# Experts of the second block's mixture: output copies, width of the weight rounding, and order of the third product's passes

## The chip, the cores and the metric

The kernel runs on one core of a Trainium2 chip. The metric is the device time of one execution in microseconds (us), as the median of several executions. TensorE (PE) multiplies, VectorE (DVE), ScalarE (ACT) and GpSimd (POOL) work on elements, and the sync engine (SP) and POOL issue transfers. [...]

## The reference

The program is two transformer blocks in a row over one sequence of 2,048 tokens with a width of 1,024, in float32. The change lies in the second block's mixture of experts, cut to what matters here:

```python
# 32 experts, D = 1024, hidden width 256, two experts for each token
h = rmsnorm(x, norm_ffn_g)
g_top, g_idx = top_k(softmax(h @ w_rg + b_rg), 1)          # one of 4 groups
e_top, e_idx = top_k(softmax(e_in), 2)                     # two of its 8 experts
wts = g_top * e_top / sum(e_top)
def expert(xb, e):
    return (silu(xb @ w_g[e]) * (xb @ w_u[e])) @ w_d[e]    # three products
x = x + sum over the token's two experts of wts * expert(h, e)
```

## The kernel before

The whole program keeps float32 precision by parts. A number is written as a high part, rounded to TensorE's short format (fp32r), and a low part, the rest. `split` (L68 to L77) makes them: ACT copies the source into the high part (L73), and a subtraction on DVE, or on POOL where it is told so, makes the low part (L74). A product is then three passes on PE, which `mm3` issues (L80 to L85): high by high (L83), high by low (L84), low by high (L85). In the rows the operand named first behind the arrow is the one that streams, so `py<-dh,al` is the pass with the low part of the activations.

`phase_k` runs the 32 experts one after the other. Each expert has a list of token rows. A tile takes its first 128 rows, and a second tile of 64 rows is run if the expert has more than 128 (experts with over 192 would go through a loop ahead, which this data doesn't enter). For each expert x there are two versions of a block in the program, and a register chooses one: the full block with the second tile, and the else block without it. In this data 16 of the 32 blocks are full: 0 to 6, 16, 17, 19, 21 to 25 and 28.

In block x stand, in the program's order:

- for a full block, the second rows' hidden layer, `hidden2`, on PE (tile `g2`, 16 passes), with its own small chain on ACT and DVE (tile `t2`, shown as `t`; L2137 to L2141);
- the first rows' hidden layer, `hidden` (tile `g1`, 24 passes of 512 columns: gate in the first 256 columns, up in the others);
- between its passes, called by `beside`: the transposes of the next expert's rows (`turn1`, L2093, two of them, each split by ACT into `xh` and by DVE into `xl`), in odd blocks also those of the next second rows (`turn2`, L2108, tile `x2`, shown as `x`), and the transposes of the last expert's hidden layer (`out_a`, L2147, split into `ah` and `al`);
- the third product of the expert before, `out_b`: two PSUM tiles `py` of 512 columns, six passes each, copied to `y` (L2160 by ACT, L2162 by DVE), which POOL then scatters to memory (L2084);
- rounding work for the next expert: `split_in` makes the parts `gh` (ACT) and `gl` (DVE) of its gate and up weights from the loaded tile `raw`, 4,096 columns in all; `split_down` makes the parts `dh` (ACT) and `dl` (POOL) of its down weights from the loaded tile `sd`, 2,048 columns in all;
- for a full block, the second rows' third product, `out2_b` (8 passes, ACT copy L2180 and DVE add L2181).

Transposes take one of three PSUM buffers `pt`, in turn. In an odd block two `turn1` and one `turn2` come ahead of `out_a`, so `out_a` must wait until the first `turn1` buffer has been read by both its copies. The parts of the weights have two slots each, so an expert's parts are written while the other slot's are multiplied. The order on each engine is settled when the program is built, by a scheduler that models it, so it need not be the order of the code. An engine runs its own list strictly in order. POOL also gathers the next experts' rows (L2081).

Of the kernel before, what the change touches and what calls it, by code (L numbers as in the profile page):

```python
# [14 lines left out]
AF = mybir.ActivationFunctionType  # L15
# [49 lines left out]
def f32(ap):  # L65
    return ap.bitcast(F32)


def split(e, hi, lo, src, scale=None, eng=None):

    nc = e.nc
    if scale is None:
        nc.scalar.activation(hi, src, AF.Copy)  # L73
        (eng or nc.vector).tensor_tensor(lo, src, f32(hi), op=ALU.subtract)  # L74
    else:
        nc.scalar.activation(hi, src, AF.Copy, scale=scale)
        nc.vector.scalar_tensor_tensor(lo, src, scale, f32(hi), op0=ALU.mult, op1=ALU.subtract)  # L77


def mm3(e, out, a, b, start, stop):  # L80

    t = e.nc.tensor
    t.matmul(out, a[0], b[0], start=start, stop=False)  # L83
    t.matmul(out, a[0], b[1], start=False, stop=False)  # L84
    t.matmul(out, a[1], b[0], start=False, stop=stop)  # L85
# [1911 lines left out]
    V.tensor_scalar(tok, ti, 1, None, op0=ALU.arith_shift_right)  # L1997


KW = 2  # L2000


def phase_k(e, last, keep, tiles):
# [9 lines left out]
    nc, tc, d = e.nc, e.tc, e.d  # L2013
# [3 lines left out]
    with ExitStack() as st:  # L2017
# [16 lines left out]
        def half(s, i):  # L2034

            return s.rearrange("p k c -> p (k c)")[:, i * 2048:(i + 1) * 2048].rearrange("p (k c) -> p k c", k=8)
# [6 lines left out]
        def load_down(x, s):  # L2043
            nc.sync.dma_start(s.rearrange("p (k a) c -> p k (a c)", k=2), d["w_down_e_2"][0, x].rearrange("(k p) c -> p k c", p=128))
# [5 lines left out]
        def load_late(i):  # L2050
            if i == 0:
                nc.sync.dma_start(wq, d["w_ple_2"][0].rearrange("(k p) c -> p k c", p=128))
            else:
                nc.sync.dma_start(xq, d["p_2"][0, 0, tiles.start * 128:tiles.stop * 128].rearrange("(t p) c -> p t c", p=128))

        def split_in(w, s, x):

            for i in range(2):
                c = slice(i * 256, i * 256 + 256)
                for k in range(0, 8, KW):  # L2060
                    k = slice(k, k + KW)
                    split(e, w[0][:, k, c], w[1][:, k, c], half(s, i)[:, k])
                    if k.stop == 8 and x < 32:
                        load_in(x, s, i)
                    elif k.stop == 8 and i == 1:
                        e.load_gate(x % 2)
                    yield

        def split_down(w, s, x):
            for k in range(2):  # L2070
                for i in range(2):
                    c = slice(i * 512, (i + 1) * 512)
                    split(e, w[0][:, k, c], w[1][:, k, c], s[:, 2 * k + i], eng=nc.gpsimd)
                    if k == i == 1 and x < 32:
                        load_down(x, s)
                    elif k == i == 1:
                        load_late(x % 2)
                    yield

        def gather(tok, xr):  # L2080
            nc.gpsimd.indirect_dma_start(out=xr, out_offset=None, in_=HF, in_offset=bass.IndirectOffsetOnAxis(ap=tok, axis=0))  # L2081
# [1 line left out]
        def scatter(y, dst):  # L2083
            nc.gpsimd.indirect_dma_start(out=Y, out_offset=bass.IndirectOffsetOnAxis(ap=dst, axis=0), in_=y, in_offset=None,  # L2084
                                         bounds_check=2 * S - 1, oob_is_err=False)
# [13 lines left out]
        def turn1(xr, x, parts=(0, 1)):  # L2099
            turn(xr, lambda j: x[0][:, 4 * j:4 * j + 4], lambda j: x[1][:, 4 * j:4 * j + 4], parts)  # L2100

        def turn2(xr, x2, parts=(0, 1)):

            for j in parts:
                p = pt.tile([128, 4, 128], F32, name="pt")
                for i in range(4):
                    k = 4 * j + i
                    nc.tensor.transpose(p[:, i, :], xr[:, k * 128:(k + 1) * 128], e.ident)  # L2108
                pv = p.rearrange("p i (e c) -> p i e c", e=2)
                h, l = (x2[:, 4 * j:4 * j + 4, :, q, :] for q in range(2))  # L2110
                split(e, h, l, pv)
# [4 lines left out]
        def hidden(w, x, sg, beside=lambda k: None):  # L2116

            g = pg.tile([128, 512], F32, name="g1")
            for k in range(8):
                mm3(e, g, (x[0][:, k], x[1][:, k]), (w[0][:, k], w[1][:, k]), k == 0, k == 7)  # L2120
                beside(k)
            nc.scalar.activation(sg, g[:, :256], AF.Silu)
            nc.vector.tensor_mul(sg, sg, g[:, 256:])
# [8 lines left out]
        def hidden2(w, x2, i):  # L2132
            g = pg.tile([128, 512], F32, name="g2")
            for k in range(8):
                both(g, x2[:, k, i], w[0][:, k], w[1][:, k], k == 0, k == 7)
            t = op.tile([64, 512], F32, name="t2", bufs=1)
            nc.scalar.activation(t, g[64:128], AF.Copy)  # L2137
            nc.vector.tensor_add(t, t, g[0:64])
            sg = t[:, :256]
            nc.scalar.activation(sg, sg, AF.Silu)  # L2140
            nc.vector.tensor_mul(sg, sg, t[:, 256:])  # L2141
            return sg

        def out_a(sg):
            p = pt.tile([128, 4, 128], F32, name="pt")
            for i in range(2):
                nc.tensor.transpose(p[:, i, :], sg[:, i * 128:(i + 1) * 128], e.ident)  # L2147
            a = [op.tile([128, 2, 128], F32R, name="a" + n) for n in "hl"]
            split(e, a[0], a[1], p[:, 0:2])
            return a  # L2150

        def out_b(w, a, dst):
            y = op.tile([128, D], F32, name="y")
            for j in range(2):
                yp = py.tile([128, 512], F32, name="py")
                c = slice(j * 512, (j + 1) * 512)
                for k in range(2):
                    mm3(e, yp, (a[0][:, k], a[1][:, k]), (w[0][:, k, c], w[1][:, k, c]), k == 0, k == 1)
                if j == 0:
                    nc.scalar.activation(y[:, c], yp, AF.Copy)  # L2160
                else:
                    nc.vector.tensor_copy(y[:, c], yp)  # L2162
            scatter(y, dst)

        def out2_a(sg):
            p = pt.tile([128, 4, 128], F32, name="pt")
            for i in range(2):
                nc.tensor.transpose(p[:, i, :64], sg[:, i * 128:(i + 1) * 128], e.ident[:64, :64])
            a = op.tile([128, 2, 2, 64], F32R, name="a2")
            split(e, a[:, :, 0], a[:, :, 1], p[:, 0:2, :64])  # L2170
            return a
# [12 lines left out]
        def all_of(g):  # L2184
            for _ in g:
                pass
# [31 lines left out]
        with tc.If(most > 1):  # L2218
            with tc.For_i(0, 32) as x:
                n = nc.values_load(nb[0:1, bass.ds(x, 1)], min_val=0, max_val=17)  # L2220
                with tc.For_i(1, n) as j:
                    xj = sb.tile([128, 2], F32, name="xj")
                    for i, r in enumerate((x, j)):
                        a = RT[bass.ds(r, 1)]
# [9 lines left out]
                    p = pt.tile([128, 4, 128], F32, name="pt")  # L2234
# [10 lines left out]
                    for name, w, k, c in (("w_gate_e_2", W[1], 4, 0), ("w_up_e_2", W[1], 4, 256), ("w_down_e_2", WD[1], 1, 0)):  # L2245
                        src = d[name][0, bass.ds(x, 1)].rearrange("o r c -> (o r) c").rearrange("(k p) c -> p k c" if k == 1 else "(p k) c -> p k c", p=128)
                        for h in range(2):
                            k_, c_ = slice(h * k, (h + 1) * k), slice(c, c + 1024 // k)
                            s = op.tile([128, D], F32, name="y").rearrange("p (k c) -> p k c", k=k)
# [9 lines left out]
        def block(x, second):  # L2259

            y = (x + 1) % 2
            steps = split_in(W[y], RG[y], x + 3) if x < 31 else iter(())
            parts = lambda n: [next(steps, None) for _ in range(n)]
            parts(2)
            if second:
                sg2 = hidden2(W[x % 2], x2, x % 2)
                parts(2)
            a, a2 = [], []

            def beside(k):  # L2270
                if k == OUT and x:
                    a.extend(out_a(SG[x - 1]))
                if k in TURN and x < 31:
                    turn1(XR[(x + 1) % 2], X[x + 1], (TURN.index(k),))
                    if k == TURN[1]:
                        rows(x + 3)
                if k == OUT2 and second:
                    a2.append(out2_a(sg2))
                if k in TURN2 and x % 2 == 1 and x < 31:
                    turn2(xr2, x2, (TURN2.index(k),))  # L2280
                    if k == TURN2[1]:
                        rows2(x // 2 + 2)
                parts(1)

            hidden(W[x % 2], X[x], SG[x], beside)
            if x:
                out_b(WD[(x - 1) % 2], a, e.dst[:, 0, x - 1:x])
            parts(16)
            if x < 31:
                all_of(split_down(WD[y], RD[y], x + 3))  # L2290
            if second:
                out2_b(WD[x % 2], a2[0], e.dst[0:64, 1, x:x + 1])
            if x == 31:
                out_b(WD[x % 2], out_a(SG[x]), e.dst[:, 0, x:x + 1])

        for x in range(32):
# [6 lines left out]
            n = nc.values_load(nb[0:1, 33 + x:34 + x], min_val=0, max_val=33)  # L2303
# [186 lines left out]
```

## Time and profile before

| | |
|---|---|
| median of 3 runs | 3558.35 us (3557.78 to 3562.14) |
| profiled execution | 3560.11 us |
| its span | 3558.4 us |
| mean granted TensorE clock | 0.975 of 2.4 GHz |
| busy share of the span | PE 94%, DVE 68%, ACT 58%, POOL 19% |
| stretch of the 32 expert blocks | 2861.7 to 3327.0 us of the span |

The profile gives busy times by engine and line, the waits (which engine sat idle at which line, and which instruction of another engine ended it), and the instructions in order of time. A row of the order of time has the start, the time from the first start to the last end of the instructions merged in it, the engine, line and operation, the tiles, and in brackets the idle time of the engine before it with what ended it.

### The profile page before, as it was taken

What the parts mean: (1) busy time and instruction counts of PE and PEld (TensorE: products, weight loads), DVE (VectorE), ACT (ScalarE), POOL (GpSimd) and SP (SyncE); (2) the same over time, 40 slices, a digit from 0 to 9 for tenths busy, and PEclk for the clock granted to TensorE, in tenths of its full rate; (3) what the DMA queues carried; (4) which work ended last, traced back from release to release, by engine and by line L of the source; (5) the groups of instructions that cost most, each with busy time, mean ns of one, the idle gap of its engine ahead of it and who ended that gap; (6) DMA issues with size and microseconds to landing.
All of it is one profiled execution on the core that took longest, in us unless ns stands there. A gap on an engine that the chain in (4) does not pass through costs nothing. (4 is left out here: it accounts for less than half of the span.)

```text
span 3558.4 us, 48779 instructions
## 1 busy us (share of the span) xinstructions
PE 3340.2 (94%) x16556; PEld 2592.6 (73%) x16557; DVE 2427.9 (68%) x4600; ACT 2052.8 (58%) x3672; POOL 688.9 (19%) x729
## 2 busy tenths in 40 slices
PE   8999999999999998999986998988999989899798
PEld 6788766666666666889975777766778767677687
DVE  5835768888888865464454887877856657877654
ACT  4442357777777783243223777877833467777533
POOL 0000000000000000000022433433200046655332
PEclk9999999999999998999997999999999989999999
DMA  5333322101111026443247533332255578878753
GB/s 160 102 122 105 95 71 72 51 22 54 34 45 44 26 63 197 146 139 112 75 127 187 106 79 77 84 69 60 83 167 167 211 263 309 342 301 302 276 195 130
DMA packets 312984, 468.82 MB, mean 132 GB/s; under 512 B 66455, under 2 KB 201384, under 8 KB 304416
## 3 DMA queue, kind: packets, MB, share of 16 engines
q1 hardware_dynamic: 293174, 404.26, 36.6%
q0 software_dynamic: 19520, 60.97, 4.7%
q8 instruction: 148, 2.42, 0.3%
q14 instruction: 142, 1.16, 0.1%
HBM read 333.81 MB, written 135.24 MB: 132 GB/s over the span
## 5 line engine op out<-in xcount | busy, mean ns | idle before, releaser
L519 DVE TENSOR_REDUCE mx<-pmx 128x1 f32<-128x512 f32 x512 | 344.5, 685 | 85.0 <-PE pmx L518 78.8
L588 DVE TENSOR_TENSOR pl<-pe,ph 128x1024 fp32r<-128x1024 f32 (+1 forms) x272 | 340.5, 1253 | 88.5 <-ACT ph L581 87.1
L579 ACT ACTIVATE pe<-ps 128x1024 f32<-128x1024 f32 (+1 forms) x272 | 278.7, 1025 | 147.2 <-PE ps L577 137.1
L581 ACT ACTIVATE ph<-pe 128x1024 fp32r<-128x1024 f32 (+1 forms) x272 | 287.4, 1058 | 7.4
L576 PE MATMUL ps<-t,kh 128*128 128x512 f32 (+1 forms) x544 | 239.6, 440 | 0.8 <-ACT pe L579 0.8
L1294 DVE TENSOR_TENSOR pl<-pe,ph 128x512 fp32r<-128x512 f32 (+1 forms) x320 | 211.6, 664 | 39.5 <-ACT ph L1287 36.9
L74 DVE TENSOR_TENSOR gl<-raw,gh 128x512 fp32r<-128x512 f32 x256 | 222.1, 915 | 19.0 <-ACT gh L73 18.6
L577 PE MATMUL ps<-t,kl 65*128 65x512 f32 (+1 forms) x544 | 222.9, 410 | 0.0
L602 PE MATMUL acc<-ph,vh 128*65 128x512 f32 (+1 forms) x544 | 217.5, 400 | 0.0
L604 PE MATMUL acc<-pl,vh 128*65 128x512 f32 (+1 forms) x544 | 215.1, 396 | 0.0
L603 PE MATMUL acc<-ph,vl 128*65 128x512 f32 (+1 forms) x544 | 215.0, 395 | 0.0
L518 PE MATMUL pmx<-kh,t 128*128 128x512 f32 x512 | 207.4, 410 | 1.7 <-DVE mx L519 1.1
L1258 DVE TENSOR_REDUCE mx<-pmx 128x1 f32<-128x512 f32 (+2 forms) x320 | 190.7, 598 | 9.1 <-PE pmx L1257 8.8
L1285 ACT ACTIVATE pe<-ps 128x512 f32<-128x512 f32 (+1 forms) x320 | 167.0, 523 | 30.7 <-PE ps L1283 27.5
L1287 ACT ACTIVATE ph<-pe 128x512 fp32r<-128x512 f32 (+1 forms) x320 | 179.5, 564 | 6.5
L74 POOL TENSOR_TENSOR dl<-sd,dh 128x512 fp32r<-128x512 f32 x128 | 165.4, 1313 | 80.4 <-ACT dh L73 77.8
L1281 PE MATMUL ps<-t,kh 113*128 113x512 f32 (+1 forms) x320 | 136.0, 425 | 35.7 <-ACT pe L1285 28.9
L83 PE MATMUL pm<-uhi,fh 128*128 128x256 f32 x512 | 146.0, 286 | 7.4 <-ACT ev L956 3.9
L73 ACT ACTIVATE gh<-raw 128x512 fp32r<-128x512 f32 x256 | 141.1, 621 | 13.0 <-PE p L85 9.4
L84 PE MATMUL pm<-ulo,fh 128*128 128x256 f32 x512 | 144.6, 283 | 0.0
L85 PE MATMUL pm<-uhi,fl 128*128 128x256 f32 x512 | 144.2, 284 | 0.3 <-DVE fl L77 0.3
L626 POOL TENSOR_TENSOR rc<-rc,ag 128x512 f32<-128x512 f32 x16 | 23.9, 1495 | 608.0 <-DMA rc<-scr_RD 561.6
(545 smaller groups left out, 9641.7 us busy)
## 6 DMA issues: line engine op xcount, KB each, us to landing
raw<-in_w_gate_e SPq DMA_DIRECT2D x32, 1024.0 KB
raw<-in_w_up_e SPq DMA_DIRECT2D x32, 1024.0 KB
sd<-in_w_down_e SPq DMA_DIRECT2D x32, 1024.0 KB
ws<-in_w_in SPq DMA_DIRECT2D x80, 256.0 KB
xt<-in_x SPq DMA_DIRECT2D x32, 512.0 KB
scr_X<-y SPq DMA_DIRECT2D x32, 512.0 KB
xt<-scr_X SPq DMA_DIRECT2D x32, 512.0 KB
yy<-scr_Y POOLq DMA_DIRECT2D x32, 512.0 KB, 4.7
```

What stands on the lines that cost most here:

```text
L74: (eng or nc.vector).tensor_tensor(lo, src, f32(hi), op=ALU.subtract)
L518: nc.tensor.matmul(p, t1[:, i * 128:(i + 1) * 128], kh[:, j * 512:(j + 1) * 512], start=True, stop=True)
L519: nc.vector.reduce_max(mx[:, i, j:j + 1], p, axis=AX.X)
L576: nc.tensor.matmul(p[:n, c], kh[:, k0:k0 + n], t1[:, c], start=True, stop=False)
L577: nc.tensor.matmul(p[:n, c], kl[:, k0:k0 + n], t2[:, c], start=False, stop=True)
L579: nc.scalar.activation(pe[:n], p[:n], AF.Exp, scale=0.125)
L581: nc.scalar.activation(ph[:n], pe[:n], AF.Copy)
L588: nc.vector.tensor_tensor(pl[:n], pe[:n], f32(ph[:n]), op=ALU.subtract)
L602: nc.tensor.matmul(A[u][j], vh[:n, i, :65], ph[:n, c], start=i == 0, stop=False)
L603: nc.tensor.matmul(A[u][j], vl[:n, i, :65], ph[:n, c], start=False, stop=False)
L604: nc.tensor.matmul(A[u][j], vh[:n, i, :65], pl[:n, c], start=False, stop=i == 16)
L1294: nc.vector.tensor_tensor(pl[:, c0:], pe[:, c0:], f32(ph[:, c0:]), op=ALU.subtract)
```

## The change

Three things change in `phase_k`. `split_in` rounds in steps of four groups of 256 columns instead of two, so each `gh` and each `gl` has 1,024 columns instead of 512, and there are four of each for an expert instead of eight. `split_down` works on 1,024 columns at a time, two `dh` and two `dl` instead of four. In `out_b` the six passes of a tile run the four with the high part of the activations first and the two with the low part last, and both tiles' copies to `y` are on ACT. The calls of `parts` are thinned so that the four steps spread over the block.

```diff
-KW = 2
+KW = 4
         def split_down(w, s, x):
             for k in range(2):
-                for i in range(2):
-                    c = slice(i * 512, (i + 1) * 512)
-                    split(e, w[0][:, k, c], w[1][:, k, c], s[:, 2 * k + i], eng=nc.gpsimd)
-                    if k == i == 1 and x < 32:
-                        load_down(x, s)
-                    elif k == i == 1:
-                        load_late(x % 2)
-                    yield
+                raw = s[:, 2 * k:2 * k + 2].rearrange("p a c -> p (a c)")
+                split(e, w[0][:, k], w[1][:, k], raw, eng=nc.gpsimd)
+                if k == 1 and x < 32:
+                    load_down(x, s)
+                elif k == 1:
+                    load_late(x % 2)
+                yield
@@ out_b
-                for k in range(2):
-                    mm3(e, yp, (a[0][:, k], a[1][:, k]), (w[0][:, k, c], w[1][:, k, c]), k == 0, k == 1)
-                if j == 0:
-                    nc.scalar.activation(y[:, c], yp, AF.Copy)
-                else:
-                    nc.vector.tensor_copy(y[:, c], yp)
+                terms = [(0, k, h) for k in range(2) for h in range(2)] + [(1, k, 0) for k in range(2)]
+                for n, (q, k, h) in enumerate(terms):
+                    nc.tensor.matmul(yp, a[q][:, k], w[h][:, k, c], start=n == 0, stop=n == 5)
+                nc.scalar.activation(y[:, c], yp, AF.Copy)
@@ block
-            parts(2)
+            parts(1)
             if second:
                 sg2 = hidden2(W[x % 2], x2, x % 2)
-                parts(2)
+                parts(1)
@@ beside
-                parts(1)
+                if k % 2:
+                    parts(1)
```

ACT in the else block of expert 10. `gh1`, `dh1`: high parts of the gate and up weights and of the down weights, slot 1; `xh`, `ah`: high parts of rows and of the hidden layer. First before, from the block's start to its end:

```order
L73 ACTIVATE gh1_28452<-raw1_28437 128x2x256 x3
L73 ACTIVATE xh_31485<-pt_31653 128x512
L73 ACTIVATE gh1_28452<-raw1_28437 128x2x256 x3
L73 ACTIVATE xh_31485<-pt_31671 128x512
L73 ACTIVATE gh1_28452<-raw1_28437 128x2x256 x2
L73 ACTIVATE ah_31692<-pt_31689 128x256
L2122 ACTIVATE sg_31487<-g1_31649 128x256
L73 ACTIVATE dh1_28456<-sd1_28459 128x512
L2160 ACTIVATE y_31712<-py_31713 128x512
L73 ACTIVATE dh1_28456<-sd1_28459 128x512 x3
```

The same list after the change:

```order
L73 ACTIVATE gh1_28452<-raw1_28437 128x4x256 x2
L73 ACTIVATE xh_31233<-pt_31387 128x512
L73 ACTIVATE gh1_28452<-raw1_28437 128x4x256 x2
L73 ACTIVATE xh_31233<-pt_31403 128x512
L73 ACTIVATE ah_31422<-pt_31419 128x256
L2121 ACTIVATE sg_31235<-g1_31383 128x256
L2160 ACTIVATE y_31440<-py_31441 128x512
L73 ACTIVATE dh1_28456<-sd1_28459 128x1024
L2160 ACTIVATE y_31440<-py_31449 128x512
L73 ACTIVATE dh1_28456<-sd1_28459 128x1024
```

The first `dh` moved from ahead of the first copy to behind it, and the second copy stands between the two. The slot that a `dh` writes is the one that `out_b` of this same block reads. In the program before, the four `dh` wait for passes 3, 6, 9 and 12 of `out_b`; after it, the two wait for passes 11 and 12.

DVE in the same block, before and then after; `gl1`, `xl`, `al` are the low parts, L2123 (L2122) the gate's multiplication:

```order
L74 TENSOR_TENSOR gl1_28453<-raw1_28437,gh1_28452 128x2x256 x3
L74 TENSOR_TENSOR xl_31486<-pt_31653,xh_31485 128x512
L74 TENSOR_TENSOR gl1_28453<-raw1_28437,gh1_28452 128x2x256 x2
L74 TENSOR_TENSOR xl_31486<-pt_31671,xh_31485 128x512
L74 TENSOR_TENSOR gl1_28453<-raw1_28437,gh1_28452 128x2x256
L74 TENSOR_TENSOR al_31693<-pt_31689,ah_31692 128x256
L74 TENSOR_TENSOR gl1_28453<-raw1_28437,gh1_28452 128x2x256 x2
L2123 TENSOR_TENSOR sg_31487<-sg_31487,g1_31649 128x256
L2162 COPY y_31712<-py_31721 128x512
```

```order
L74 TENSOR_TENSOR gl1_28453<-raw1_28437,gh1_28452 128x4x256 x2
L74 TENSOR_TENSOR xl_31234<-pt_31387,xh_31233 128x512
L74 TENSOR_TENSOR gl1_28453<-raw1_28437,gh1_28452 128x4x256
L74 TENSOR_TENSOR xl_31234<-pt_31403,xh_31233 128x512
L74 TENSOR_TENSOR al_31423<-pt_31419,ah_31422 128x256
L74 TENSOR_TENSOR gl1_28453<-raw1_28437,gh1_28452 128x4x256
L2122 TENSOR_TENSOR sg_31235<-sg_31235,g1_31383 128x256
```

Ahead of the first `xl` stood 1,536 columns of `gl` and stand 2,048 now; ahead of `al` stood 3,072 and stand 3,072. The copy of `y` is gone from the end. In full blocks all of `gl` stands ahead of the first `xl`, before and after.

POOL in the same block, before and then after; L2081 (L2080) gathers rows, L2084 (L2083) scatters the output:

```order
L2081 DMA xr1_28512<-scr_HF,tok_26230 128x1024
L74 TENSOR_TENSOR dl1_28457<-sd1_28459,dh1_28456 128x512 x3
L2084 DMA scr_Y<-y_31712,dst_26231 4096x1024
L74 TENSOR_TENSOR dl1_28457<-sd1_28459,dh1_28456 128x512
```

```order
L2080 DMA xr1_28500<-scr_HF,tok_26230 128x1024
L74 TENSOR_TENSOR dl1_28457<-sd1_28459,dh1_28456 128x1024
L2083 DMA scr_Y<-y_31440,dst_26231 4096x1024
L74 TENSOR_TENSOR dl1_28457<-sd1_28459,dh1_28456 128x1024
```

Behind the scatter stood 512 columns of `dl` and stand 1,024 now.

## Rows read from the trace of the kernel before

**Rows 1.** Expert stretch: us; busy us of PE, PEld, DVE, ACT, POOL; clock; DMA.

```profile
2861.70:3327.00 465.30, 428.80 (x2002) 325.41 (x2002) 352.16 (x516) 330.82 (x647) 266.85 (x219) 0.98 0.80 298
```

**Rows 2.** Waits of PE in that stretch: us in total, times, longest us.

```profile
PE pt L2147 <- DVE xl L74: 15.9, 12, 1.9
PE py L85 <- DVE al L74: 11.9, 8, 2.2
```

**Rows 3.** Groups of instructions: count, busy us, mean ns, idle before and its releaser.

```profile
L588 DVE TENSOR_TENSOR pl<-pe,ph 128x1024 fp32r<-128x1024 f32 (+1 forms) x272 | 340.5, 1253 | 88.5 <-ACT ph L581 87.1
L581 ACT ACTIVATE ph<-pe 128x1024 fp32r<-128x1024 f32 (+1 forms) x272 | 287.4, 1058 | 7.4
L2408 POOL TENSOR_TENSOR raw<-raw,x 128x1024 f32<-128x1024 f32 x2 | 4.8, 2410 | 3.0 <-DVE raw L2407 2.9
L626 POOL TENSOR_TENSOR rc<-rc,ag 128x512 f32<-128x512 f32 x16 | 23.9, 1495 | 608.0 <-DMA rc<-scr_RD 561.6
```

**Rows 4.** Order of time, DVE, block 10 (an else block behind an else block).

```profile
3019.42 0.69 DVE L2162 COPY y<-py 128x512 f32<-128x512 f32 x1 [0.56 <-PE py L85]
3020.88 4.43 DVE L74 TENSOR_TENSOR gl<-raw,gh 128x512 fp32r<-128x512 f32 x3 [0.77 <-ACT gh L73]
3025.23 0.68 DVE L74 TENSOR_TENSOR xl<-pt,xh 128x512 fp32r<-128x512 f32 x1
...
3028.24 0.41 DVE L74 TENSOR_TENSOR al<-pt,ah 128x256 fp32r<-128x256 f32 x1
```

**Rows 5.** Order of time, ACT, the same block.

```profile
3018.08 0.60 ACT L2160 ACTIVATE y<-py 128x512 f32<-128x512 f32 x1
3018.57 1.66 ACT L73 ACTIVATE dh<-sd 128x512 fp32r<-128x512 f32 x3
3020.15 1.68 ACT L73 ACTIVATE gh<-raw 128x512 fp32r<-128x512 f32 x3
```

**Rows 6.** Order of time, POOL, the same block.

```profile
3018.18 3.80 POOL L74 TENSOR_TENSOR dl<-sd,dh 128x512 fp32r<-128x512 f32 x3 [1.06 <-ACT dh L73]
3022.13 1.28 POOL L2084 DMA_INDIRECT scr_Y<-y,dst  x1
3023.43 1.32 POOL L74 TENSOR_TENSOR dl<-sd,dh 128x512 fp32r<-128x512 f32 x1
```

**Rows 7.** Order of time, PE, blocks 10 and 11 (start of each, and its wait).

```profile
3019.22 0.40 PE L83 MATMUL g<-gh,xh 128*128 128x512 f32 x1
...
3028.70 0.50 PE L85 MATMUL py<-dh,al 128*128 128x512 f32 x1 [2.18 <-DVE al L74]
...
3031.09 0.39 PE L83 MATMUL g<-gh,xh 128*128 128x512 f32 x1
...
3037.95 0.64 PE L2147 MATMUL pt<-ident,sg 128*128 128x128 f32 x2 [1.92 <-DVE xl L74]
```

**Rows 8.** Order of time, block 23 (odd, full): PE, DVE, POOL.

```profile
3201.61 0.39 PE L2127 MATMUL g<-gh,x 128*128 128x512 f32 x1
...
3211.07 0.44 PE L2147 MATMUL pt<-ident,sg 128*128 128x128 f32 x2 [0.81 <-DVE xl L74]
...
3203.18 6.04 DVE L74 TENSOR_TENSOR gl<-raw,gh 128x512 fp32r<-128x512 f32 x7
...
3202.72 0.99 POOL L2084 DMA_INDIRECT scr_Y<-y,dst  x1
3203.72 1.33 POOL L74 TENSOR_TENSOR dl<-sd,dh 128x512 fp32r<-128x512 f32 x1
```

**Rows 9.** Order of time, PE: block 22 (even, full), block 26 (else behind full).

```profile
3186.15 0.39 PE L2127 MATMUL g<-gh,x 128*128 128x512 f32 x1
...
3196.66 0.33 PE L2168 MATMUL pt<-ident,t 64*128 64x64 f32 x2
...
3251.50 0.39 PE L2127 MATMUL py<-dh,a 128*128 128x512 f32 x1
...
3260.36 0.50 PE L85 MATMUL py<-dh,al 128*128 128x512 f32 x1 [0.51 <-DVE al L74]
```

## The prediction

> **What bounds the kernel now.** The stretch of the 32 expert blocks comes first, since the change touches nothing else: 465.30 us, of which PE is busy 428.80 [rows 1]. So 36.5 us of PE's idle time are all that could be won there, and whatever is lost must appear as idle time of PE. Then PE's waits in that stretch: 15.9 us in 12 waits until `xl` is written on DVE, so that `out_a` gets its buffer, and 11.9 us in 8 waits at the third pass of `out_b` until `al` is written on DVE [rows 2]. PE thus waits for DVE alone that much, and in both cases for an instruction that stands behind `gl` in DVE's list. The order of time says when that list begins. In block 10, which starts at 3019.22 [rows 7], ACT does three `dh` until 3020.23, starts `gh` at 3020.15, .93 after the block's start [rows 5], and DVE starts `gl` at 3020.88, +1.66 [rows 4]. Three `gl` then take 4.43 us. The reason stands on POOL: `dl` runs until 3021.98, a scatter from 3022.13, and the last `dl` from 3023.43 to 3024.75 [rows 6]. The third `gl` ends at 3025.31, .56 behind that `dl`; so a `gl` that is caught by a `dl` ends .56 after it. In block 23 the first `gl` starts at 3203.18, ahead of the `dl` at 3203.72 but behind the scatter's start at 3202.72, and is caught too: seven take 6.04 us [rows 8]. Both ends of the chain that bounds a block are then known: ACT must finish `dh` before `gh` begins, and DVE's `gl` must get past POOL's last `dl` before `xl` and `al` come.
>
> **The change, part by part.** I write S for the start of PE's first pass in a block. A pass takes .23 to .24 (ten from 3028.70 to 3031.09 [rows 7]).
>
> *Prices.* ACT with 1,024 columns takes 1.06 and DVE's subtraction with 1,024 takes 1.25 [rows 3]. On POOL a 1,024-column one takes 2.41, one of 512 in another place 1.50, and the 512-column `dl` 1.32 [rows 3, 6]; by that step of .91 the new `dl` takes 2.23, by twice the old one 2.64. I take 2.3, the nearer to the row of the same width, and keep both ends. Two instructions in a row of the same engine overlap by about .1 (ACT, DVE). Cost removed: on ACT six instructions less for about .1 each, and one copy of .60 more [rows 5], so nothing; on DVE four less and the copy of .69 [rows 4], about 1 us a block. That only counts if DVE's list begins no later than now.
>
> *ACT, else block behind an else block.* Now the `dh` run while `out_b` still runs. Afterwards the first must wait for pass 11, which starts S-.48; the copy of `y`, behind pass 12, started at 3019.42, .44 after that pass [rows 4], so `dh` runs from S-.04 to 1.02, the second copy to 1.51, the second `dh` from 1.40 to 2.46, and `gh` from 2.35 to 3.41 instead of from .93. `gl` begins at 3.50 instead of 1.66. What is queued behind the later `dh` is thus the whole rounding of the next expert.
>
> *POOL.* First `dl` from 1.10 to 3.40, scatter from 3.55 with 1.14 (between 1.28 and .99 [rows 6, 8]) to 4.69, second `dl` 4.70 to 7.00.
>
> *DVE.* The first `gl` runs 3.50 to 4.75. The second begins at 4.67, meets the `dl` and ends after it by .56 plus the .57 by which it is longer: 8.13. Then `xl` to 8.73, `gl` to 9.90, `xl` to 10.50, `al` to 10.83. Now `al` ended at 3028.65, +9.43 [rows 4].
>
> *The sum by kinds of block.*
> Even else blocks behind an else block (8, 10, 12, 14, 30): PE gets to the first pass with `al` at 10.88 instead of 9.48 (3028.70 [rows 7]); that pass is now the fifth instead of the third, which gives back .48: +.9 each, +4.5.
> Odd else blocks behind an else block (9, 11, 13, 15, 27): `out_a` waits for the first `xl`. In block 11 it went at 3037.95, 6.86 after the start at 3031.09, with a wait of 1.92 [rows 7]. It will go at 8.8: +1.9 each, +9.5. `al`, some 2 us later, is then in time.
> Odd full blocks (8 of them): here eight passes of `out2_b` lie between `out_b` and the end, so pass 11 is at S-2.4, the `dh` run from -1.95 to -.90 and -.5 to .55, the two copies L2180 to 1.5, `gh` from 1.45, `gl` ready at 2.6. POOL: `dl` -.8 to 1.5, scatter (.99) to 2.65, `dl` to 4.95. The first `gl` is caught and ends at 6.08, the others at 7.25, 8.42 and 9.6, `t` at 10.2, `xl` at 10.8. `out_a` goes at 10.85 instead of 9.46 (3211.07 less 3201.61 [rows 8]): +1.4 each, +11.2. For a cross-check of the two odd kinds: without a wait `out_a` would go at 4.94 and 8.65, so the new waits are 5 x 3.86 and 8 x 2.2, in all 36.9, less the 15.9 of [rows 2], which is +21.0; the two terms give +20.7.
> Even full blocks (7, without block 0): no `turn2`, so `out_a` has its buffer; but `t`'s last step on DVE, behind `xl`, ends at 11.15, and the transposes that need it (L2168) went at 3196.66, 10.51 after 3186.15 [rows 9]: +.7 each, +4.9.
> Else blocks behind a full one (7, 18, 20, 26, 29): counted from where the block would start, .23 after 3251.50 [rows 9], the chain is that of the full blocks: second `gl` 7.25, `xl` 7.85, `gl` 9.0, `xl` 9.6, `al` 10.0. Three even ones: 10.05 instead of 8.63 (3260.36 [rows 9]), less .48: +.95 each. Two odd ones: `out_a` at 7.9 instead of about 5.7: +2.2 each. Together +7.3.
> In all 4.5 + 9.5 + 11.2 + 4.9 + 7.3 = **+37.4 us**. The first block, whose `dh` and `dl` for expert 1 now start ahead of it, can win, and the last one, with later outputs, lose; I take 0, from -4 to +2.5. The granted clock is .98 in the stretch [rows 1]; I add nothing for it, and up to 9 at the top of the range, since longer waits of PE could lower it more often.
> The profiled execution, 3560.1, becomes 3597.5; it lies 1.8 over the median of 3558.35, so the forecast is **3596 us** for the median. With a `dl` of 2.23 it is 4 us less; with 2.64 each of the two adds .34 in 31 blocks: 3617.
>
> **The rivals.**
> *Faster, 3542 us.* POOL yields: its second `dl` waits until a row of `gl` is through, and DVE's list runs unhindered. Then the full blocks' `gl` end at 3.85, 5.0, 6.2 and 7.3 and `xl` at 8.6, in time; else blocks have `xl` at 6.5 and `al` at 8.8. Even else blocks gain 1.1 each (8: -9), odd ones and odd full ones about .3 to .8 (13: -7): -16. It decides from the point at which `gl` stands behind no `dl`. Against it: all `gl` caught in the rows shown ended behind the `dl`, even one that started ahead of it [rows 8].
> *Worse, 3618 us.* In the else blocks the first `gl` starts at 3.50, just about when the scatter starts (3.55). In block 23 a `gl` that began .46 after the scatter's start was caught by the `dl` behind it [rows 8]. If `gh` comes .3 later than I think or the scatter earlier, the first `gl` is caught as well, ends at 8.13, and everything behind it comes 1.17 later in ten else blocks: +12; with half of the clock's 9, or a `dl` nearer to 2.64, 3612 to 3628.
> *No change, 3558 us.* The catches fall half the one way and half the other, and the 1 us of DVE work a block pays for the later start.
>
> The Trainium skill ("SBUF — State Buffer", section "Who interferes with whom") says that issue order decides which of DVE and GpSimd blocks the other. By that rule the `gl` of block 23 would have gone first; the trace shows seven `gl` in 6.04 us, 1.8 more than seven of about .6, so that the `dl` issued later went first, and the row and not the rule is used [rows 8]. By the rule the worse rival, in which a `dl` that is issued later catches a `gl` already begun, could not happen, and its chance would go to the forecast.
>
> **How the numbers follow.** Forecast's mechanism (3578 to 3612): .62. Worse: .18. Faster: .12. No change: .08. A measurement of this kernel can tell about 0.2%, 7 us, from no change: faster .12, same .08, slower .80. The range leaves out the faster rival and the top of the worse one (.08): 3556 to 3622.
>
> **What would show it.** In the new profile: `gh` begins 2.3 us after the start of an else block instead of .9; `dl` takes 2.2 to 2.4 with the second one right behind the scatter; the second `gl` of else blocks and the first of full blocks take over 3 us; PE's waits for `xl` at `out_a` rise from 15.9 to about 37 us, and none for L2160 appears. If `gh` begins before +1.5, or the mean `gl` of 1,024 columns is near 1.25, the forecast is wrong and the time is near or under 3558.

## Result, and the profile after

The change makes the kernel slower: 3605.93 us (median of 4, 3602.73 to 3609.07) against 3560.24 us for the kernel before on the same chip, a ratio of 1.013 (95% interval 1.0108 to 1.0152), or +45.7 us. The forecast was 3596 with 3556 to 3622, and slower with .80. The profiled execution took 3602.73 us with a span of 3600.9.

The stretch of the expert blocks, from PE's first pass of block 0 to its last of block 31, answers to [rows 1] (columns: stretch, us, busy us of PE, PEld, DVE, ACT and POOL with counts, granted clock, DMA):

```profile
2864.80:3367.40 502.60, 435.62 (x2002) 329.99 (x2002) 323.97 (x361) 323.15 (x489) 285.75 (x155) 0.96 0.72 276
```

It grew from 465.3 to 502.6 us, +37.3. PE's idle time in it rose from 36.5 to 67.0 (+30.5), and PE's busy time for the same 2,002 instructions by 6.8, at a granted clock of .96 instead of .98. The span as a whole is 42.5 us longer; the other 5 us lie in the phases ahead of the stretch and behind it, which the change doesn't touch: in the profiles of all the kernels below the stretch begins anywhere from 2860.5 to 2872.8. So I compare stretches below, beside the times.

PE's waits in it (us in total, times, longest us), to be held against [rows 2]:

```profile
PE pt L2146 <- DVE xl L74: 25.9, 12, 2.9
PE g L83 <- ACT gh L73: 13.0, 5, 2.6
PE pt L2166 <- DVE t L2140: 7.5, 8, 1.8
PE pt L2107 <- DVE xl L74: 7.5, 5, 1.5
PE py L2159 <- DVE al L74: 7.1, 5, 1.4
```

The wait for `xl` at `out_a` went from 15.9 to 25.9, and a second one for `xl` appears at the second `turn2` (L2107, 7.5). The wait for `al` shrank from 11.9 to 7.1. The second row is that of the first pass of an else block behind a full one. Before, the same five waits were two rows:

```profile
PE g L83 <- DVE y L2181: 2.3, 4, 0.6
PE g L83 <- ACT gh L73: 1.7, 1, 1.7
```

The groups of the two subtractions and of the scatter (count, busy us, mean ns, idle before), and below them `gl` and the scatter of the kernel before:

```profile
L74 DVE TENSOR_TENSOR gl<-raw,gh 128x1024 fp32r<-128x1024 f32 x124 | 206.3, 1703 | 70.1 <-ACT gh L73 44.7 <-issue 25.4
L74 POOL TENSOR_TENSOR dl<-sd,dh 128x1024 fp32r<-128x1024 f32 x64 | 155.7, 2434 | 138.5 <-ACT dh L73 138.2
L2083 POOL DMA_INDIRECT scr_Y<-y,dst x47 | 63.1, 1342 | 25.8 <-issue 11.4 <-DVE y L2179 5.4 <-DVE gl L74 3.1
...
L74 DVE TENSOR_TENSOR gl<-raw,gh 128x512 fp32r<-128x512 f32 x248 | 216.9, 923 | 19.0 <-ACT gh L73 18.6
L2084 POOL DMA_INDIRECT scr_Y<-y,dst x47 | 53.9, 1147 | 50.2 <-DVE gl L74 20.5 <-DVE xl L74 7.9 <-DVE t L2141 6.9
```

Block 10 in order of time (start, us, engine, line, operation, tiles; the block starts at 3030.87), ACT, then DVE, POOL and PE; it answers to [rows 4 to 7]:

```profile
3030.89 1.06 ACT L73 ACTIVATE dh<-sd 128x1024 fp32r<-128x1024 f32 x1 [0.53 <-PE py L2159]
3031.86 0.58 ACT L2160 ACTIVATE y<-py 128x512 f32<-128x512 f32 x1
3032.34 1.05 ACT L73 ACTIVATE dh<-sd 128x1024 fp32r<-128x1024 f32 x1
3033.29 1.04 ACT L73 ACTIVATE gh<-raw 128x1024 fp32r<-128x1024 f32 x1
...
3034.42 2.36 DVE L74 TENSOR_TENSOR gl<-raw,gh 128x1024 fp32r<-128x1024 f32 x2 [4.53 <-ACT gh L73]
3036.70 0.69 DVE L74 TENSOR_TENSOR xl<-pt,xh 128x512 fp32r<-128x512 f32 x1
3037.30 2.81 DVE L74 TENSOR_TENSOR gl<-raw,gh 128x1024 fp32r<-128x1024 f32 x1
3040.03 0.68 DVE L74 TENSOR_TENSOR xl<-pt,xh 128x512 fp32r<-128x512 f32 x1
3040.64 0.41 DVE L74 TENSOR_TENSOR al<-pt,ah 128x256 fp32r<-128x256 f32 x1
...
3032.03 2.40 POOL L74 TENSOR_TENSOR dl<-sd,dh 128x1024 fp32r<-128x1024 f32 x1 [2.26 <-ACT dh L73]
3034.59 1.93 POOL L2083 DMA_INDIRECT scr_Y<-y,dst  x1 [0.16 <-issue]
3036.54 2.49 POOL L74 TENSOR_TENSOR dl<-sd,dh 128x1024 fp32r<-128x1024 f32 x1
...
3030.87 0.40 PE L83 MATMUL g<-gh,xh 128*128 128x512 f32 x1
...
3038.47 0.50 PE L2159 MATMUL py<-dh,ah 128*128 128x512 f32 x1 [0.75 <-ACT ah L73]
...
3041.10 0.73 PE L2159 MATMUL py<-dh,al 128*128 128x512 f32 x2 [1.43 <-DVE al L74]
```

ACT is as forecast: `dh` at +.02 (forecast -.04), `gh` at +2.42 (2.35), DVE's `gl` at +3.55 (3.50). What follows is not: the second `gl` isn't caught. Two take 2.36, the scatter beside them takes 1.93 instead of 1.28, and only then comes the `dl`, from +5.67 to +8.16, which catches the third (2.81 instead of 1.2). So the first `xl` ends at +6.52 and not at 8.73.

### The profile page after: what moved, and what is told of

Read it like the earlier page. It is cut to its first block, busy times and chain, and to the rows that moved or that the text cites. A ratio compares the mean times of both kernels' runs of the same rounds, so it can differ in the third digit from the quotient of the medians.

```text
span 3600.9 us, 48170 instructions
## 1 busy us (share of the span) xinstructions
PE 3348.9 (93%) x16556; PEld 2598.9 (72%) x16557; DVE 2397.3 (67%) x4440; ACT 2046.8 (57%) x3512; POOL 706.6 (20%) x665
## 3 DMA queue, kind: packets, MB, share of 16 engines
q8 instruction: 148, 2.42, 0.3%
## 5 line engine op out<-in xcount | busy, mean ns | idle before, releaser
L74 DVE TENSOR_TENSOR gl<-raw,gh 128x1024 fp32r<-128x1024 f32 x128 | 211.1, 1688 | 70.2 <-ACT gh L73 44.7
L74 POOL TENSOR_TENSOR dl<-sd,dh 128x1024 fp32r<-128x1024 f32 x64 | 155.7, 2434 | 138.5 <-ACT dh L73 138.2
L538 POOL DMA_DIRECT2D t<-nm x16 | 9.2, 572 | 682.3 <-DMA scr_AG<-ev 445.8
```

## Experiments

All ran against the kernel before on the same chip. Times are medians, ratios with their 95% interval; "stretch" is the length of the expert stretch in the profiled execution less the 465.3 of the kernel before. Each stretch comes from one execution, and what it would vary by in another was not measured, so a few us between two stretches decide nothing.

**The four parts, each alone.** My theory was that the later `dh` and the long `dl` cost, the rival that the coarse `gl` does.

Wide `dh` and `dl` alone: the new `split_down`, nothing else.

> Kernel before with the down weights alone rounded by 1,024 columns (two dh, two dl). Theory, late rounding and long dl: dh then waits for passes 9 and 12 instead of 3, 6, 9 and 12, so gh begins some .5 us later in an else block (+1.4 instead of +.93), and the dl behind the scatter lasts 2.4 instead of 1.3 us, so that the gl it catches comes 1.1 later. Expected +10 to +25 us, PE's wait for xl at out_a above 20 us. Rival, coarse gl (the wide gl alone costs): within 5 us of before.

Measured: 3615.8 us, ratio 1.0149 (1.0132 to 1.0167), stretch +55.8. This part alone costs more than the whole change, and twice the top of what I expected.

Wide `gh` and `gl` alone:

```diff
-KW = 2
+KW = 4
```

with the thinned calls of `parts`.

> Kernel before with the gate and up weights alone rounded by 1,024 columns (four gh, four gl for an expert). Theory, late rounding and long dl: gh still begins at +.93, the dl are as before; ahead of the first xl stand 2,048 columns instead of 1,536 in else blocks, and the saved instructions give back .25 us: between -5 and +8 us. Rival, coarse gl: +20 us or more, over half of the 37 us that the whole change costs in the expert stretch.

Measured: 3547.53 us, ratio 0.9959 (0.9938 to 0.9980), stretch -21.1. The rival falls: this part is a gain, and a larger one than I allowed. PE's waits in this kernel:

```profile
PE pt L2147 <- DVE xl L74: 9.4, 13, 1.0
PE py L85 <- DVE al L74: 5.7, 8, 1.2
```

Both are about half of [rows 2]. Block 10 of this kernel shows why: two `gl` of 1,024 columns take 2.94 us, and the scatter between the third and fourth `dl` stretches to 1.8, so that POOL's last `dl` comes when the two are through; before, three `gl` of 512 took 4.43 for fewer columns [rows 4]. Over the whole stretch 1,024 columns of `gl` take 1,496 ns here and took 2 x 923 before. By the kernels without catches below (2 x 704 against 1,221), some half of that gain is the saved instruction and the other half fewer catches; this is an estimate and was not tried by itself.

The order of the passes alone:

```diff
-                for k in range(2):
...
+                terms = [(0, k, h) for k in range(2) for h in range(2)] + [(1, k, 0) for k in range(2)]
...
```

> Kernel before with the passes with the low part of the activations put last in out_b, all else as before (the second copy on DVE, 512-column rounding). Theory: the even else blocks, where PE waited at the third pass for al, gain up to .48 us each (8 blocks, -4); against it three of the four dh now wait for pass 11, so gh begins some .6 us later: odd else and full blocks lose up to .6 each. Expected between -4 and +10 us. Rival, coarse gl: -4 us.

Measured: 3569.13 us, ratio 1.0015 (1.0001 to 1.0029), stretch +5.4: inside what I expected, and hardly clear of no change.

Both copies on ACT alone:

```diff
-                if j == 0:
-                    nc.scalar.activation(y[:, c], yp, AF.Copy)
-                else:
-                    nc.vector.tensor_copy(y[:, c], yp)
+                nc.scalar.activation(y[:, c], yp, AF.Copy)
```

> Kernel before with both output copies on ACT, all else as before. Theory: ACT has .5 us more to do between the last pass of out_b and gh, so gh begins at +1.4 instead of +.93 and DVE's missing copy (.69) is no gain, since DVE waited there anyway: +5 to +15 us. Rival, that DVE's work is what bounds a block: -5 to -15 us.

Measured: 3566.57 us, ratio 1.0004 (0.9991 to 1.0017), stretch +1.8. No change can be told, neither the loss that I expected nor a gain from DVE's free copy. The four stretches add to +41.9, near the +37.3 of the whole change.

**What in the wide `dh` and `dl` costs.** Two kernels split that part: `dh` alone by 1,024 (four `dl` of 512), and `dl` alone by 1,024 (four `dh` of 512).

```diff
+                nc.scalar.activation(w[0][:, k], raw, AF.Copy)
...
+                    nc.gpsimd.tensor_tensor(w[1][:, k, c], s[:, 2 * k + i], f32(w[0][:, k, c]), op=ALU.subtract)
```

> Kernel before with dh alone by 1,024 columns on ACT (two for an expert), dl on POOL still four of 512. The later wait of dh is then there without the longer dl. If the later start of gh and gl is what costs in the kernel with wide dh and dl (54 us over before): +35 us or more. If the dl of 1,024 columns cost, each catching a gl for twice as long behind the scatter: +0 to +15 us.

Measured: 3652.48 us, ratio 1.0247 (1.0227 to 1.0268), stretch +78.8. That is worse than both widths together, so it can't be the price of the later `gh` alone. The order of POOL's list tells what else moved: the scheduler put the scatter behind the first `dl` and three `dl` behind the scatter. In block 10 they ran as one piece of 3.80 us, and three `gl` took 5.95 us. The run is thus no clean test of the later `gh`.

```diff
...
+                    nc.scalar.activation(w[0][:, k, c], s[:, 2 * k + i], AF.Copy)
+                nc.gpsimd.tensor_tensor(w[1][:, k], raw, f32(w[0][:, k]), op=ALU.subtract)
```

> Kernel before with dl alone by 1,024 columns on POOL (two for an expert, the first behind two dh), dh on ACT still four of 512, so that gh begins at +.93 as before. If the long dl cost: +35 us or more. If the later start of gh costs: +5 to +15 us.

Measured: 3607.08 us, ratio 1.0123 (1.0100 to 1.0147), stretch +43.5. Here ACT is as before. Block 10 starts at 3028.33; ACT, DVE and POOL in order of time:

```profile
3029.27 1.14 ACT L73 ACTIVATE gh<-raw 128x512 fp32r<-128x512 f32 x2
...
3029.98 5.84 DVE L74 TENSOR_TENSOR gl<-raw,gh 128x512 fp32r<-128x512 f32 x3 [0.76 <-ACT gh L73]
3035.74 0.68 DVE L74 TENSOR_TENSOR xl<-pt,xh 128x512 fp32r<-128x512 f32 x1
...
3028.99 2.40 POOL L2075 TENSOR_TENSOR dl<-sd,dh 128x1024 fp32r<-128x1024 f32 x1 [2.72 <-issue]
3031.55 1.27 POOL L2086 DMA_INDIRECT scr_Y<-y,dst  x1 [0.16 <-DMA scr_Y<-y,dst]
3032.84 2.43 POOL L2075 TENSOR_TENSOR dl<-sd,dh 128x1024 fp32r<-128x1024 f32 x1
```

`gh` begins at +.94 and `gl` at +1.65, as before, yet three `gl` take 5.84 instead of 4.43, since the `dl` behind the scatter ends at +6.94 instead of +5.53. The long `dl` is enough to cost 43 us when `gl` goes in pieces of 512.

**Taking the catches away.** In two kernels, the one before and the changed one, the `dl` subtractions are left out for all but the first two experts; PE makes as many passes, with stale low parts.

```diff
-            (eng or nc.vector).tensor_tensor(lo, src, f32(hi), op=ALU.subtract)
+        if part:
+            (eng or nc.vector).tensor_tensor(lo, src, f32(hi), op=ALU.subtract)
```

> Kernel before without the dl subtractions on POOL for all experts but the first two (the low parts of the other experts' down weights are left out of the computation; PE multiplies the stale ones, in as many passes). Theory, that a gl caught by a dl is what makes PE wait for xl and al: the three gl of block 10 take 1.9 instead of 4.4 us, PE's waits in the stretch (36.5 us) fall below 15: -20 to -30 us against before. Rival, that PE waits because ACT begins gh late and not because of the catches: -5 to +2 us.

Measured: 3527.74 us, ratio 0.9894 (0.9871 to 0.9917), stretch -36.7. The mean `gl` of 512 fell from 923 to 704 ns, PE's idle time to 10.5 us:

```profile
L75 DVE TENSOR_TENSOR gl<-raw,gh 128x512 fp32r<-128x512 f32 x248 | 161.6, 704 | 22.3 <-ACT gh L73 21.9
```

That is more than I expected: nearly all of the kernel's waits for `xl` and `al` hung on POOL's subtractions.

> The changed kernel with the same left out (no dl on POOL for all experts but the first two). Theory: gh still begins at about +2.4 in else blocks, but no gl is caught, xl comes at about +6: +0 to +15 us against the kernel before without dl, so under 3570 us, 35 us or more under the changed kernel. Rival, late ACT: still 25 us or more over the kernel before without dl.

Measured: 3561.27 us, ratio 0.9980 (0.9966 to 0.9994), stretch -4.8. That is 42 us under the changed kernel's stretch, but 31.9 us over that of the kernel before without `dl`. Here the rival holds: with no `gl` caught, the changed kernel still costs more. PE's waits, first of the kernel before without `dl`, then of the changed one without:

```profile
PE pt L2148 <- DVE xl L75: 1.8, 2, 1.3
```

```profile
PE pt L2147 <- DVE xl L75: 13.6, 12, 1.6
PE g L84 <- ACT gh L73: 12.7, 5, 2.5
```

`xl` comes too late in 12 blocks although no subtraction runs on POOL. Of the 31.9 us, 13.6 lie in the five else blocks behind a full one, where the second row stands.

**The scatter behind all four `dl`** (kernel before, POOL's order alone):

```diff
+            if x:
+                with (tc.issue_after(lastdl[0].ins) if x < 31 else ExitStack()):
+                    put()
```

> Kernel before with POOL's scatter of the first rows' output behind all four dl of a block instead of ahead of the last one; nothing else moves. Theory: the fourth dl then ends about 1.3 us sooner and no gl is caught behind a scatter; full blocks' first gl ends 1 us sooner, else blocks' third gl 1 to 1.4: -8 to -20 us. Rival, that the scatter between gives DVE its turn, and four dl in a row hold it off as long in all: -3 to +5 us.

Measured: 3578.63 us, ratio 1.0031 (1.0018 to 1.0045), stretch +13.3. Neither the gain I expected nor the few us of the rival. In block 10 three `gl` took 4.00 instead of 4.43. Most of the loss, 5.2 us each, lies in the two odd full blocks behind an else block, 19 and 21. In block 21 (POOL, then DVE):

```profile
3170.45 0.91 POOL L2084 DMA_INDIRECT scr_Y<-y,dst  x1 [6.40 <-DMA scr_Y<-y,dst]
3171.66 0.96 POOL L2081 DMA_INDIRECT xr<-scr_HF,tok  x1 [0.30 <-issue]
3172.65 5.04 POOL L74 TENSOR_TENSOR dl<-sd,dh 128x512 fp32r<-128x512 f32 x4
...
3172.28 9.58 DVE L74 TENSOR_TENSOR gl<-raw,gh 128x512 fp32r<-128x512 f32 x7 [0.69 <-ACT gh L73]
```

POOL stood 6.40 us ahead of a scatter, by the row until an earlier one into the same tensor had landed. So its four `dl` came late and in one piece, and the first `gl`, begun .37 ahead of them, ended .55 behind the last: seven took 9.58 us instead of 6.91. PE waited 4.37 for `xl` instead of 1.70. That is half of the 5.2 us. The other half is the clock, granted at .50, that is 1.2 GHz, in the stretch around the end of this wait (columns as above):

```profile
3182.91:3189.74 6.83, 6.03 (x18) 4.49 (x19) 3.30 (x7) 2.53 (x6) 0.95 (x1) 0.50 1.03 424
```

The loss is thus again a catch, by another run of `dl`; what the scatter's place alone is worth the run doesn't tell.

**Undoing one part of the change, and a better version.** The changed kernel with four `dh` and four `dl` again:

> The changed kernel with the down weights rounded by 512 columns again (four dh, four dl); wide gh and gl, the pass order and both copies on ACT stay. If the parts' prices simply add (wide gh and gl -15, order +5, copies +2): about -8, 3550 to 3563 us. If the later gh that order and copies cause takes the gain of the wide gl away: 3563 to 3580 us.

Measured: 3562.85 us, ratio 0.9994 (0.9980 to 1.0008), stretch -10.1. The wide down weights are the change's loss: without them it is level with the kernel before. The other parts together give 11 us less than the wide `gl` alone in the stretch, and 15 us less in the time. The time lies on the border between my two expectations and doesn't decide between them.

The changed kernel with its two `dl` on DVE:

```diff
-                split(e, w[0][:, k], w[1][:, k], raw, eng=nc.gpsimd)
+                split(e, w[0][:, k], w[1][:, k], raw)
```

> The changed kernel with its two 1,024-column dl on DVE instead of POOL; all is computed. No subtraction of POOL is left for a gl to be caught by. If the later start of gh costs by itself, as the two kernels without dl say (33 us apart): 3555 to 3575 us, some 30 over the kernel with wide gl, narrow dh and dl on DVE. If only the catches cost: 3525 to 3540 us.

Measured: 3557.72 us, ratio 0.9987 (0.9971 to 1.0003), stretch -8.7. And the same `dl` on DVE, with the wide `gh` and `gl` but with 512-column `dh` and `dl`, the old order and the old copies:

> Wide gh and gl as in the change, 512-column dh, pass order and copies as before, and the dl subtractions on DVE instead of POOL. If a DVE and a POOL subtraction hold each other up, DVE gets 4 x .6 us more work in a block of 10 to 17 us, and no wait on POOL is left: 3520 to 3540 us, under both kernels. If DVE's work itself bounds the else blocks: 3550 us or more.

Measured: 3532.77 us, ratio 0.9911 (0.9891 to 0.9930), stretch -36.4: faster than both kernels, with everything computed. Its subtractions and its largest waits for DVE's low parts:

```profile
L74 DVE TENSOR_TENSOR gl<-raw,gh 128x1024 fp32r<-128x1024 f32 x124 | 146.1, 1221 | 7.0 <-ACT gh L73 6.2
L74 DVE TENSOR_TENSOR dl<-sd,dh 128x512 fp32r<-128x512 f32 x128 | 85.2, 688 | 25.1 <-ACT dh L73 24.6 <-PE py L84 0.5
```

```profile
PE pt L2147 <- DVE xl L74: 3.1, 6, 0.5
PE py L85 <- DVE al L74: 1.3, 6, 0.3
```

DVE does 85 us more, `gl` are never held up (1,221 ns instead of 1,703), and PE is idle 9.9 us in all. Against the kernel with the wide `gl` alone the move is worth 15 us of the stretch. Between the two kernels with `dl` on DVE lie 27.7 us of stretch: the wide `dh` and `dl`, the order and the copies, with no subtraction on POOL. 13.0 of them lie in the five else blocks behind a full one. It is near the 31.9 without `dl`, by another way.

## Why the prediction was right, and where its steps were off

**The mechanism held.** PE's idle time carries most of the loss, 30.5 of 37.3 us, through DVE's low parts. DVE's list begins 1.9 us later in block 10 because two 1,024-column `dh` and a copy stand between the last passes of `out_b` and `gh`; the times were met to .07 us. That the change costs without any catch is shown twice, by the pair without `dl` (31.9) and by the pair with `dl` on DVE (27.7). Both also hold the later first pass of the else blocks behind full ones; what the later `gl` costs by itself was not separated. That catches of `gl` by `dl` cost is shown by the long `dl` alone (+43.5) and by leaving the `dl` out (-36.7 and -42). Since the catches cost nearly as much before the change as after it, only some 5 of the +37.3 come from more catching; the larger part is there without any, and my sum had not told the two apart.

**The sum, +37.4, met the stretch, +37.3, by luck.** It was a sum of PE's waits alone, and these grew by 30.5; the clock, which I had left out, made up the rest. By kinds, forecast and measured (block lengths of before and after in the two profiles, and how much of each is idle time of PE):

| blocks | forecast | measured | of it idle |
|---|---|---|---|
| 5 even else behind else | +4.5 | -0.4 | +0.4 |
| 5 odd else behind else | +9.5 | +6.5 | +8.0 |
| 8 odd full | +11.2 | +13.4 | +9.5 |
| 7 even full, without block 0 | +4.9 | +7.0 | +6.0 |
| 5 else behind full, with the wait at their first pass | +7.3 | +12.3 | +7.5 |
| first and last block | 0 (-4 to +2.5) | -1.5 | -0.9 |

The first pass of an else block behind a full one waited 2.59 us each of five times, against .57 in four and 1.66 in one of before; that wait is counted with the else block in the table.

**Which `gl` is caught** is the step that failed in else blocks. I let the second `gl` meet the `dl`. On the chip DVE went on with its next `gl` while the scatter stretched, which is what the faster rival supposed; the third, which began .76 behind the `dl`, was caught. So the `al` of block 10 ended at +10.18 instead of 10.83. With two more passes ahead of it PE waited 1.43 for it and .75 for `ah`, in all as long as the 2.18 before [rows 7], and the waits of the even blocks grew by .4 and not by 4.5. In full blocks the first `gl` is caught as forecast: in block 17 four take 7.08, and PE's `out_a` waited 2.40 (forecast 2.2).

**Odd else blocks** waited twice for `xl` where I had one wait: in block 11 at `out_a` for 1.62, and at the second `turn2` for 1.49.

**The else block behind a full one** waited as much as forecast (+7.5 against +7.3), but at another place: at its first pass, a wait that I had folded into its chain. In block 17, DVE's adds of the second rows' output and PE's first pass of the next block:

```profile
3146.03 1.28 DVE L2179 TENSOR_TENSOR y<-y,py 64x512 f32<-64x512 f32 x2 [4.97 <-ACT y L2178]
...
3147.46 0.47 PE L83 MATMUL g<-gh,xh 128*128 128x512 f32 x1 [2.59 <-ACT gh L73]
```

The adds stand behind ACT's two copies, and these behind the second wide `dh`. The row names `gh`, but PE starts .15 behind the end of the second add. At the same place PE started .15 behind the first of two adds in the kernel before, and .14 behind the second `dl`, ahead of both adds, in the changed kernel with `dl` on DVE:

```profile
3127.59 0.68 DVE L2181 TENSOR_TENSOR y<-y,py 64x512 f32<-64x512 f32 x1 [0.85 <-ACT y L2180]
...
3128.42 0.47 PE L83 MATMUL g<-gh,xh 128*128 128x512 f32 x1 [0.57 <-DVE y L2181]
```

```profile
3124.00 1.23 DVE L74 TENSOR_TENSOR dl<-sd,dh 128x1024 fp32r<-128x1024 f32 x1 [0.20 <-ACT dh L73]
3125.14 1.27 DVE L2178 TENSOR_TENSOR y<-y,py 64x512 f32<-64x512 f32 x2
...
3125.37 0.47 PE L83 MATMUL g<-gh,xh 128*128 128x512 f32 x1 [1.87 <-DVE dl L74]
```

So PE waits there until DVE has come to some point of its list, and not for the adds as such; what it needs from DVE stays open.

**Wide `gl`** I had costed at nothing beyond the .1 of each saved instruction. Alone it is worth -21.1 in the stretch, and wide `dh` and `dl` alone cost +55.8. Neither price stood in my sum; only what they make together did. For each part alone, costed in the same way, the middle of what I expected missed the stretch by some 20 and by some 40 us.

**The `dl`** takes 2.43 us; I took 2.3, and the nearer row of the same width, 2.41, would have been right.

**The clock** cost 6.8 us of PE's busy time, inside the 0 to 9 that I kept for the top of the range and left out of the sum. It shows in single stretches. In block 26 PE's first pass began at 3284.80 behind a wait of 2.59, and soon after the clock was granted at .50:

```profile
3286.19:3289.60 3.41, 3.41 (x11) 2.77 (x11) 3.41 (x3) 2.58 (x4) 2.33 (x2) 0.50 0.50 131
```

Behind the same wait in block 18 it stayed at 1.00. Such stretches are also why the even blocks come out at -.4: before, blocks 8 and 12 had one, and after it block 30.

That the time came out 10 us over the forecast has other reasons: 5 us lie in phases that the change doesn't touch, and the median lies 3 us over the profiled execution, where I had put it 1.8 under.

**The rule on issue order** of the Trainium skill ("SBUF — State Buffer", section "Who interferes with whom") fits the else blocks of the changed kernel, where the second `gl`, begun ahead of the `dl`, went first. It doesn't fit the full blocks, where the first `gl` of block 17, started at 3128.52, was held by a `dl` that the profile starts at 3128.65 (DVE and POOL in order of time; four `gl` undisturbed take some 4.6):

```profile
3128.52 7.08 DVE L74 TENSOR_TENSOR gl<-raw,gh 128x1024 fp32r<-128x1024 f32 x4 [0.16 <-ACT gh L73]
...
3127.64 1.01 POOL L2083 DMA_INDIRECT scr_Y<-y,dst  x1 [0.15 <-ACT y L2178]
3128.65 2.45 POOL L74 TENSOR_TENSOR dl<-sd,dh 128x1024 fp32r<-128x1024 f32 x1
```

Both happen behind a scatter on POOL; what decides between them stays open.

## What to carry to other kernels

Where two engines can hold each other up, cost a wider instruction not by its saved overhead but by how long it holds the other engine and by what stands ahead of it in its engine's list: here the same widening was worth -21 us on DVE and +43 us on POOL. A rounding that waits for the last reader of its buffer should be narrow, or stand behind whatever the next stage waits for; the first fits the changed kernel with narrow `dh` and `dl`, where the `dl` is narrow as well, and the second was not tried. Before tuning pieces, try the contended work on the engine that it contends with: 128 subtractions moved from POOL to DVE, with the wide `gl`, gave 34 us against the kernel before, of which the wide `gl` alone gave 15.

## What the runs showed of the hardware that was not expected

POOL's scatter is itself held up beside two DVE subtractions of 1,024 columns: 1.93 us in block 10 against 1.28 before, and 1,342 ns in the mean of 47 against 1,147. In the changed kernel's block 10 a `gl` that followed another without a gap went through beside it and the `dl` came after; in block 17 a `gl` that began alone, .88 us into a scatter, was held until the `dl` behind it ended.
